# Second attention of a two-layer trunk: dividing by the softmax sums ahead of the transposes

## The chip, the cores and the metric

The kernel runs on one core of a Trainium2 chip. Its engines work from queues of their own, in order, and wait for each other by semaphores: TensorE (PE) multiplies matrices and transposes, VectorE (DVE) and ScalarE (ACT) do elementwise work, GpSimd (POOL) takes some of it, and SyncE (SP) starts transfers. The metric is the device time of one execution in microseconds (us), as the median of several runs.

## The reference

Two layers over 512 positions of width 1024; each has a token mixer and a gated MLP. The change is in the second layer's mixer, attention with 16 heads over a shared latent of width 128, limited to the 128 keys that an indexer picks for each query:

```python
def block(args):
    ...
    _, sel = lax.top_k(isc, topk)
    kg = k[bidx, sel]
    vg = vals[bidx, sel]
    logits = jnp.einsum('bqhd,bqkd->bqhk', qb, kg) * scale
    logits = logits + jnp.swapaxes(bias, -1, -2)
    logits = jnp.where(valid[:, :, None, :], logits, NEG)
    p = jax.nn.softmax(logits, axis=-1)
    return jnp.einsum('bqhk,bqkd->bqhd', p, vg)
...
o = jnp.einsum('bshl,hlv->bshv', o_lat, w_uv)
return o.reshape(B, S, DSA_HEADS * DSA_V_DIM) @ w_out
```

## The kernel before

The kernel keeps 512 positions on chip and streams the weights. Float32 products are made of three matmuls on split operands (a high and a low part). The second attention goes head by head. Queries of a head lie in four blocks j of 128, and block j needs only the first (j + 1) * 128 keys, so its tile `L[h, j]` has 128, 256, 384 or 512 columns.

For a head and a block these steps follow each other:

- `masked_bias` writes the scaled position bias into `L` (on ACT, on POOL for the two narrow blocks, on DVE for head 1) and POOL adds the mask (L1408). It runs two heads ahead.
- `logits` makes three matmuls into a PSUM tile `z` (L1421 to L1423).
- `softmax` adds `z` to `L` on DVE, with the row's least value as `nm` (L1431, two instructions: the operation and the read of its accumulator).
- `expo` takes the exponential on ACT in place and leaves the row sums in `sum` (L1436).
- `transposed` turns `L` on TensorE so that keys lie on partitions, in three groups: `tr` number 0 takes the first key block of all four tiles, number 1 and number 2 the rest (L1446). ACT copies number 0 into `pT` (L1451), DVE copies numbers 1 and 2 (L1453).
- `pair_values` projects the latent to the values of two heads, `weighted` multiplies a pair's transposed exponentials with them into the PSUM tile `av`, 64 partitions for each head (L1477).

The division by the sums comes last, for a pair of heads together. `av` has the value's columns on partitions and queries along the row, so the reciprocals have to lie along the row as well: `sums` takes the reciprocals, `pair_sums` spreads them over 64 columns on DVE (`rvb`, L1482), `pair_scale` transposes them in four matmuls (`bc`, L1491) and copies them to `bs` on ACT (L1493). `pair_hi` multiplies `av` by `bs` on DVE (L1497) and takes the high part on ACT (`ohi`, L1500); `pair_lo` subtracts for the low part on DVE (`olo`, L1504). The output projection uses both.

The order is the order in which the code is written; each engine's queue keeps it. Iteration h of the head loop makes logits and exponentials of head n = h + 1 and transposes head h, so `tr` of head h + 1 is the first use of what iteration h made. Between them `fill(k)` puts k steps (three matmuls of 512 columns each) of work from elsewhere, projections of the late heads' queries and later the output projection; `LATE_STEPS` says how many at three places of each iteration. In even iterations from 2 on, `weighted` of the pair before comes between the logits and the first transposes; in odd ones the first transposes follow right behind two blocks of logits.

Of the kernel before, what the change touches and what calls it, by code (L numbers as in the profile page):

```python
# [9 lines left out]
F32 = mybir.dt.float32  # L10
# [111 lines left out]
def kernel_body(ctx, tc, xT, wst, cst, smalls, crow, ccol, relb, onehot, outT):  # L122
# [959 lines left out]
    def dsa_layer(l, first, man):  # L1082
        with ExitStack() as st:
# [252 lines left out]
            with ExitStack() as sa:  # L1336
# [73 lines left out]
                def begin(h):  # L1410
                    if h % 2 == 0:
                        rv = ap.tile([P, QT, 2], F32, name="rv", bufs=4)
                        heads["rv"] = rv
                    heads[h] = (ap.tile([P, QT], F32, name="nm"), ap.tile([P, QT], F32, name="sum"), heads["rv"], {})

                def logits(h, j):
                    qh, ql = Q[h]
                    ns = (j + 1) * P
                    qs = slice(j * P, ns)
                    z = heads[h][3][j] = ptile([P, S], "z", "z")  # L1420
                    pe.matmul(z[:, :ns], lhsT=qh[:, qs], rhs=kph[:, :ns], start=True, stop=False)  # L1421
                    pe.matmul(z[:, :ns], lhsT=ql[:, qs], rhs=kph[:, :ns], start=False, stop=False)
                    pe.matmul(z[:, :ns], lhsT=qh[:, qs], rhs=kpl[:, :ns], start=False, stop=True)  # L1423

                def softmax(h, j):

                    nm, sum_, rv, z = heads[h]
                    z, L = z.pop(j), Ls[h, j]
                    ns = (j + 1) * P
                    c = h * QT + j  # L1430
                    dve.tensor_tensor_reduce(L, z[:, :ns], L, rq[:, c:c + 1], -USED, op0=OP.add, op1=OP.min,  # L1431
                                             accum_out=nm[:, j:j + 1])
# [47 lines left out]
                def pair_sums(rv):  # L1480
                    rvb = ap.tile([P, QT, 2, 64], F32, name="rvb", tag="bs")
                    dve.tensor_reduce(rvb, rv[:, :, :, None, None].to_broadcast([P, QT, 2, 64, 1]), axis=AX.X, op=OP.max)  # L1482
                    return rvb

                pair = {}

                def pair_scale(rvb):

                    bc = ptile([P, S], "bc", "x")
                    for j in range(QT):  # L1490
                        pe.transpose(bc[:, j * P:(j + 1) * P], rvb[:, j].rearrange("p a b -> p (a b)"), ident)  # L1491
                    bs = pair["bs"] = ap.tile([P, S], F32, name="bs")
                    act.activation(bs, bc, AF.Copy)  # L1493

                def pair_hi():
                    bs = pair["bs"]
                    dve.tensor_mul(bs, pair["av"], bs)  # L1497
                    oh = pp.tile([P, S], F32R, name="ohi", tag="qh", bufs=QRING)
                    ol = pp.tile([P, S], F32R, name="olo", tag="ql", bufs=QRING)
                    act.activation(oh, bs, AF.Copy)  # L1500
                    O.append((oh, ol))

                def pair_lo():
                    dve.tensor_sub(O[-1][1], pair["bs"], O[-1][0].bitcast(F32))  # L1504
# [14 lines left out]
                rvb = None  # L1519

                def sums(h):

                    dve.reciprocal(heads[h][2][:, :, h % 2], heads[h][1])
                    return pair_sums(heads[h][2]) if h % 2 else None

                for h in range(HEADS):
# [13 lines left out]
                    if more:  # L1540
                        softmax(n, 1)
                        expo(n, 1)
                    else:
                        rvb = sums(h)
                        pair_values(h - 1)
# [15 lines left out]
                    if values:  # L1561
                        pair_scale(rvb)
                    if more:
# [3 lines left out]
                        rvb = sums(h)  # L1567
# [10 lines left out]
                    if values:  # L1578
                        pair_hi()
                    elif h > 1:  # L1580
                        pair_lo()
                    fill(LATE_STEPS[h][2])
# [3 lines left out]
                    if not more:  # L1586
                        pair_scale(rvb)
# [135 lines left out]
```

## Time and profile before

| what | value |
|---|---|
| median of 3 runs | 1254.97 us (1254.44 to 1255.18) |
| profiled execution | 1254.88 us, its span from first to last instruction 1253.1 us |
| granted TensorE clock | 1.000 |
| busy: TensorE | 1241.6 us (99% of the span) |
| busy: weight loads of TensorE | 1015.6 us (81%) |
| busy: DVE | 929.8 us (74%) |
| busy: ACT | 607.4 us (48%) |
| busy: POOL | 119.7 us (10%), almost all between 743 and 854 us |

The second attention fills the stretch from about 743 to 866 us. A row of the timeline gives the start, the duration, the engine, the line, the operation, output and inputs with their shape, a count, and in brackets how long the engine had idled and for what. Successive operations of one engine may overlap by some hundredths of a microsecond, since a row begins before the row ahead has ended.

### The profile page before, as it was taken

Reading aid. Unit: us, or ns where it says so; the run is one execution under the profiler, and the core shown is the slowest. Engines: PE = TensorE matmul, PEld = TensorE weight load, DVE = VectorE, ACT = ScalarE, POOL = GpSimd, SP = SyncE. Lnnn points to the kernel's source line nnn. Section 1 sums busy time; section 2 is a strip of 40 time slices with the busy share of each in tenths; the row PEclk is TensorE's granted clock in tenths of the full one; section 3 lists DMA queues with packets and bytes.
Section 4 is the critical chain, followed back from the end, with each engine's and each line's share of the span. In section 5 each row is a group of like instructions: output and inputs, shape, how many; then the busy total and the mean of one; then the engine's idle time right before and its main releaser. Section 6 shows DMA issues by size and latency. Waiting matters only on the chain.

```text
span 1253.1 us, 16458 instructions
## 1 busy us (share of the span) xinstructions
PE 1241.6 (99%) x6138; PEld 1015.6 (81%) x6138; DVE 929.8 (74%) x1505; ACT 607.4 (48%) x1035; POOL 119.7 (10%) x127
## 2 busy tenths in 40 slices
PE   8999999999999999999999999999999999999998
PEld 5888787788888888888888778777888888888887
DVE  5889999798777877887788986666985455456653
ACT  6476676465323423343456447875654234234430
POOL 0000000000000000000001357773000000000000
PEclk9999999999999999999999999999999999999999
DMA  9734454413575576666322311141322422432231
GB/s 369 229 122 142 135 168 135 169 53 104 198 252 187 180 248 225 202 206 221 110 69 71 98 51 52 52 151 52 101 93 76 135 92 76 119 96 90 74 93 67
DMA packets 51327, 168.05 MB, mean 134 GB/s; under 512 B 6272, under 2 KB 7040, under 8 KB 51248
## 3 DMA queue, kind: packets, MB, share of 16 engines
q1 hardware_dynamic: 50816, 166.22, 40.9%
q8 instruction: 48, 0.79, 0.3%
q10 hardware_dynamic: 432, 0.79, 0.2%
q14 instruction: 31, 0.25, 0.1%
HBM read 164.84 MB, written 2.15 MB: 133 GB/s over the span
## 4 chain that ended last, share of the span: by engine, by line
PE 91%; DVE 4%; DMA 2%; ACT 1%; issue 1%; SPq 0%; DVEq 0%; POOL 0%; ACTq 0%
PE pt_u L252 12%; PE pt_u L253 12%; PE pt_u L254 12%; PE pt_d L253 5%; PE pt_d L252 5%; PE pt_d L254 5%; PE pt_q L252 2%; PE pt_l L252 2%; PE pt_l L254 2%; PE pt_l L253 2%; PE pt_q L254 2%; PE pt_q L253 2%; PE pt_first L252 2%; PE pt_first L254 2%; PE pt_first L253 2%; PE av L1477 1%
## 5 line engine op out<-in xcount | busy, mean ns | idle before, releaser
L211 ACT ACTIVATE whi<-raw 128x1024 fp32r<-128x1024 f32 (+1 forms) x206 | 205.0, 1002 | 110.4 <-PE pt_d L254 80.3
L252 PE MATMUL pt_u<-hhi,whi 128*128 128x512 f32 x640 | 249.2, 389 | 0.0
L253 PE MATMUL pt_u<-hhi,wlo 128*128 128x512 f32 x640 | 249.0, 389 | 0.0
L254 PE MATMUL pt_u<-hlo,whi 128*128 128x512 f32 x640 | 249.0, 389 | 0.0
L220 DVE TENSOR_TENSOR wlo<-raw,whi 128x1024 fp32r<-128x1024 f32 (+1 forms) x188 | 216.1, 1151 | 10.0 <-ACT whi L211 8.9
L995 ACT ACTIVATE y<-pt_u,sm 128x512 f32<-128x512 f32 x80 | 61.9, 777 | 180.5 <-PE pt_u L254 180.5
L252 PEld LDWEIGHTS pt_u<-hhi,whi 128*128 128x128 f32 x640 | 120.1, 188 | 26.1 <-issue 1.1
L254 PEld LDWEIGHTS pt_u<-hlo,whi 128*128 128x128 f32 x640 | 120.1, 188 | 24.9
L253 PEld LDWEIGHTS pt_u<-hhi,wlo 128*128 128x128 f32 x640 | 120.1, 188 | 24.8
L1000 DVE SCALAR_TENSOR_TENSOR y<-pt_u,sm,y 128x511 f32<-128x511 f32 x80 | 59.8, 748 | 92.7 <-ACT y L995 92.5
L254 PE MATMUL pt_d<-actlo,whi 128*128 128x512 f32 x288 | 112.0, 389 | 0.0
L252 PE MATMUL pt_d<-acthi,whi 128*128 128x512 f32 x288 | 112.0, 389 | 0.0
L253 PE MATMUL pt_d<-acthi,wlo 128*128 128x512 f32 x288 | 112.0, 389 | 0.0
L286 DVE SCALAR_TENSOR_TENSOR raw<-raw,cond 128x1024 f32<-128x1024 f32 x88 | 106.5, 1216 | 4.7 <-DMA raw<-wst 4.7
L371 DVE SCALAR_TENSOR_TENSOR x<-pt_d,mod,x 128x512 f32<-128x512 f32 x48 | 36.0, 749 | 67.1 <-PE pt_d L254 67.1
L236 ACT ACTIVATE acthi<-y 128x512 fp32r<-128x512 f32 x40 | 25.3, 632 | 94.2 <-DVE y L1018 94.2
L252 PEld LDWEIGHTS pt_d<-acthi,whi 128*128 128x128 f32 x288 | 54.1, 188 | 11.3
L254 PEld LDWEIGHTS pt_d<-actlo,whi 128*128 128x128 f32 x288 | 54.1, 188 | 11.2
L253 PEld LDWEIGHTS pt_d<-acthi,wlo 128*128 128x128 f32 x288 | 54.1, 188 | 11.2
L1001 DVE SCALAR_TENSOR_TENSOR y<-pt_u,sm,y 128x510 f32<-128x510 f32 x80 | 59.9, 749 | 2.8
L1431 DVE CUSTOM_DVE_ANT_0 L<-z,L,cols 128x128 f32<-128x128 f32 (+1 forms) x64 | 34.6, 547 | 32.2 <-PE tr L1446 22.0
L1201 POOL MEMSET work<- 128x128 f32 (+2 forms) x3 | 0.9, 308 | 585.8 <-PE pt_first L254 585.8
(307 smaller groups left out, 2561.2 us busy)
## 6 DMA issues: line engine op xcount, KB each, us to landing
raw<-wst SPq DMA_DIRECT2D x256, 512.0 KB, 3.7
raw<-wst SPq DMA_DIRECT2D x48, 384.0 KB, 3.1
th<-rb SPq DMA_DIRECT2D x16, 256.0 KB, 3.4
ada<-wst SPq DMA_DIRECT2D x4, 512.0 KB, 6.4
shrow<-shd SPq DMA_DIRECT2D x3, 512.0 KB, 3.7
outT<-x SPq DMA_DIRECT2D x6, 256.0 KB, 2.0
x<-xT SPq DMA_DIRECT2D x5, 256.0 KB, 5.1
x<-xT ACTq DMA_DIRECT2D x3, 256.0 KB, 3.9
```

What stands on the lines that cost most here:

```text
L211: act.activation(hi[:, :n], raw[:, :n], AF.Copy)
L220: engine.tensor_sub(lo[:, :w], raw[:, :w], hi[:, :w].bitcast(F32))
L236: act.activation(hi, src, AF.Copy)
L252: pe.matmul(out, lhsT=whi, rhs=ahi, start=start, stop=False)
L253: pe.matmul(out, lhsT=wlo, rhs=ahi, start=False, stop=False)
L254: pe.matmul(out, lhsT=whi, rhs=alo, start=False, stop=stop)
L286: dve.scalar_tensor_tensor(raw, raw, 1.0, cond, op0=OP.mult, op1=OP.mult, accum_out=dst)
L371: dve.scalar_tensor_tensor(x[f][:, c], pt, mod[l][:, g * KT + f:g * KT + f + 1], x[f][:, c], op0=OP.mult, op1=OP.add)
L995: act.activation(y, pt, AF.Identity, scale=cw[2], bias=sm[:, b + S_CB + c:b + S_CB + c + 1])
L1000: dve.scalar_tensor_tensor(y[:, 1:], pt[:, :S - 1], cw[1], y[:, 1:], op0=OP.mult, op1=OP.add)
L1001: dve.scalar_tensor_tensor(y[:, 2:], pt[:, :S - 2], cw[0], y[:, 2:], op0=OP.mult, op1=OP.add)
L1431: dve.tensor_tensor_reduce(L, z[:, :ns], L, rq[:, c:c + 1], -USED, op0=OP.add, op1=OP.min, accum_out=nm[:, j:j + 1])
```

## The change

The exponentials of a head are multiplied by the reciprocals of their sums on DVE, in place, before TensorE transposes them (`normed`). The reciprocals then are one number for each partition, and the spreading, its transposes, its copy and the product at the end of a pair fall away. `av` is split directly: `pair_hi` reads it from PSUM and moves to the place where `pair_scale` was, `pair_lo` follows in the same iteration. `normed` runs for the three narrow tiles behind the widest block's exponential, for the widest tile at the end of the iteration, and for all four tiles of head 0 ahead of the loop. `sum` gets four buffers.

```diff
                 def begin(h):
-                    if h % 2 == 0:
-                        rv = ap.tile([P, QT, 2], F32, name="rv", bufs=4)
-                        heads["rv"] = rv
-                    heads[h] = (ap.tile([P, QT], F32, name="nm"), ap.tile([P, QT], F32, name="sum"), heads["rv"], {})
+                    heads[h] = (ap.tile([P, QT], F32, name="nm"), ap.tile([P, QT], F32, name="sum", bufs=4), {})
...
-                def pair_sums(rv):
-                    rvb = ap.tile([P, QT, 2, 64], F32, name="rvb", tag="bs")
-                    dve.tensor_reduce(rvb, rv[:, :, :, None, None].to_broadcast([P, QT, 2, 64, 1]), axis=AX.X, op=OP.max)
-                    return rvb
-
                 pair = {}
 
-                def pair_scale(rvb):
-
-                    bc = ptile([P, S], "bc", "x")
-                    for j in range(QT):
-                        pe.transpose(bc[:, j * P:(j + 1) * P], rvb[:, j].rearrange("p a b -> p (a b)"), ident)
-                    bs = pair["bs"] = ap.tile([P, S], F32, name="bs")
-                    act.activation(bs, bc, AF.Copy)
-
                 def pair_hi():
-                    bs = pair["bs"]
-                    dve.tensor_mul(bs, pair["av"], bs)
...
-                    act.activation(oh, bs, AF.Copy)
+                    act.activation(oh, pair["av"], AF.Copy)
                     O.append((oh, ol))
 
                 def pair_lo():
-                    dve.tensor_sub(O[-1][1], pair["bs"], O[-1][0].bitcast(F32))
+                    dve.tensor_sub(O[-1][1], pair["av"], O[-1][0].bitcast(F32))
+
+                def normed(h, js):
+
+                    sum_ = heads[h][1]
+                    c = slice(js[0], js[-1] + 1)
+                    dve.reciprocal(sum_[:, c], sum_[:, c])
+                    for j in js:
+                        dve.tensor_scalar(Ls[h, j], Ls[h, j], sum_[:, j:j + 1], None, op0=OP.mult)
...
-                rvb = None
-
-                def sums(h):
-
-                    dve.reciprocal(heads[h][2][:, :, h % 2], heads[h][1])
-                    return pair_sums(heads[h][2]) if h % 2 else None
+                normed(0, range(QT))
 
                 for h in range(HEADS):
...
                     else:
-                        rvb = sums(h)
                         pair_values(h - 1)
...
                     if values:
-                        pair_scale(rvb)
+                        pair_hi()
                     if more:
                         logits(n, 3)
                         softmax(n, 3)
                         expo(n, 3)
-                        rvb = sums(h)
+                        normed(n, range(QT - 1))
...
                     if values:
-                        pair_hi()
-                    elif h > 1:
                         pair_lo()
+                    if more:
+                        normed(n, [QT - 1])
...
-                    if not more:
-                        pair_scale(rvb)
```

The order of the instructions shows three places. Names carry buffer numbers here; `L0` to `L3` are a head's four tiles, 128 to 512 columns wide. The queues of POOL and SP keep their order.

DVE in iteration 2, from the last logits step of head 3 to the first two of head 4. Before:

```order
L1431 ISA L3_6818,nm_6833<-z_6899,L3_6818,cols_5657 128x512
L1431 ISA nm_6833 128x1
L1523 RECIPROCAL rv_6748<-sum_6750 128x4
L1453 COPY pT_6859<-tr_6906 128x256
L1497 TENSOR_TENSOR bs_6897<-av_6845,bs_6897 128x512
L1431 ISA L0_6868,nm_6934<-z_6936,L0_6868,cols_5657 128x128
```

And now:

```order
L1428 ISA L3_6827,nm_6844<-z_6906,L3_6827,cols_5657 128x512
L1428 ISA nm_6844 128x1
L1492 RECIPROCAL sum_6845<-sum_6845 128x3
L1494 TENSOR_SCALAR L0_6779<-L0_6779,sum_6845 128x128
L1494 TENSOR_SCALAR L1_6800<-L1_6800,sum_6845 128x256
L1494 TENSOR_SCALAR L2_6824<-L2_6824,sum_6845 128x384
L1450 COPY pT_6870<-tr_6916 128x256
L1486 TENSOR_TENSOR olo_6904<-av_6856,ohi_6903 128x512
L1492 RECIPROCAL sum_6845<-sum_6845 128x1
L1494 TENSOR_SCALAR L3_6827<-L3_6827,sum_6845 128x512
L1428 ISA L0_6879,nm_6942<-z_6944,L0_6879,cols_5657 128x128
```

The widest multiply, which the first transposes of head 3 need, stands behind three multiplies, the copy of the last transposes and `olo`; the product with `bs` is gone.

DVE at the start, from head 0's last logits step to head 1's first. Before:

```order
L1431 ISA L3_6606,nm_6612<-z_6656,L3_6606,cols_5657 128x512
L1431 ISA nm_6612 128x1
L1403 TENSOR_SCALAR L3_6664<-th01_6512,cols_5657 128x512
L1431 ISA L0_6622,nm_6670<-z_6672,L0_6622,cols_5657 128x128
L1431 ISA nm_6670 128x1
```

And now:

```order
L1428 ISA L3_6606,nm_6611<-z_6655,L3_6606,cols_5657 128x512
L1428 ISA nm_6611 128x1
L1403 TENSOR_SCALAR L3_6663<-th01_6512,cols_5657 128x512
L1492 RECIPROCAL sum_6612<-sum_6612 128x4
L1494 TENSOR_SCALAR L0_6597<-L0_6597,sum_6612 128x128
L1494 TENSOR_SCALAR L1_6600<-L1_6600,sum_6612 128x256
L1494 TENSOR_SCALAR L2_6603<-L2_6603,sum_6612 128x384
L1494 TENSOR_SCALAR L3_6606<-L3_6606,sum_6612 128x512
L1428 ISA L0_6621,nm_6674<-z_6676,L0_6621,cols_5657 128x128
```

A reciprocal and four multiplies have come ahead of head 1's first logits step, and head 0's first transposes need them.

ACT in iteration 2, around the exponential of head 3's widest tile. Before:

```order
L1436 ACTIVATE L2_6815,sum_6834<-L2_6815,nm_6833 128x384
L1493 ACTIVATE bs_6897<-bc_6892 128x512
L1436 ACTIVATE L3_6818,sum_6834<-L3_6818,nm_6833 128x512
L1407 ACTIVATE L2_6910<-th_6732,cols_5657 128x384
L1407 ACTIVATE L3_6913<-th_6732,cols_5657 128x512
L1500 ACTIVATE ohi_6919<-bs_6897 128x512
```

And now:

```order
L1433 ACTIVATE L2_6824,sum_6845<-L2_6824,nm_6844 128x384
L1482 ACTIVATE ohi_6903<-av_6856 128x512
L1433 ACTIVATE L3_6827,sum_6845<-L3_6827,nm_6844 128x512
L1407 ACTIVATE L2_6920<-th_6739,cols_5657 128x384
L1407 ACTIVATE L3_6923<-th_6739,cols_5657 128x512
```

`ohi` has taken the place of the copy of `bs`, ahead of the exponential.

More of the change, by code (lines that the diff above doesn't have):

```diff
@@ L1419, in logits @@
                     qs = slice(j * P, ns)
-                    z = heads[h][3][j] = ptile([P, S], "z", "z")
+                    z = heads[h][2][j] = ptile([P, S], "z", "z")
                     pe.matmul(z[:, :ns], lhsT=qh[:, qs], rhs=kph[:, :ns], start=True, stop=False)
@@ L1425, in softmax @@
                 def softmax(h, j):
-                    nm, sum_, rv, z = heads[h]
+                    nm, sum_, z = heads[h]
                     z, L = z.pop(j), Ls[h, j]
```

## The prediction

> **What bounds the kernel now.** I read the table of windows first, to see which engine is full in the stage that the change touches. Columns: stretch, its length, busy time and count of TensorE (PE), its weight loads, VectorE (DVE), ScalarE (ACT), GpSimd (POOL), then granted clock and DMA.
>
> ```profile
> core 0: us, PE busy (x) PEld busy (x) DVE busy (x) ACT busy (x) POOL busy (x), PEclk, DMA share, GB/s
> 740.00:752.00 12.00, 10.29 (x59) 8.27 (x56) 8.99 (x30) 6.70 (x20) 8.09 (x11) 1.00 0.15 44
> 752.00:866.00 114.00, 113.19 (x718) 90.12 (x717) 74.93 (x205) 82.18 (x204) 80.39 (x89) 1.00 0.25 76
> ```
>
> From 752 to 866 us the second attention runs, and TensorE lacks 0.8 us of being always busy at full clock. So an operation taken off TensorE there is worth its own time, and any new wait of TensorE is lost at full price. Other engines have slack as a sum; what matters is when each hands over to TensorE.
>
> The chain of work and the group of the transposes price what is removed (start, time on the chain; group: busy us, mean ns):
>
> ```profile
> 766.33 0.44 PE bc L1491 x4
> L1491 PE MATMUL bc<-cons,rvb 128*128 128x128 f32 x32 | 4.8, 272 | 0.0
> ```
>
> Then I read the timeline, engine by engine, where one head hands over to the next. This is iteration 2, which makes head 3's exponentials while it transposes head 2; the last ACT rows and the POOL row start the bias of head 4. The 774 and 775 rows are an odd iteration, taken for spacing.
>
> ```profile
> 767.61 0.75 DVE L1431 CUSTOM_DVE_ANT_0 L<-z,L,cols 128x512 f32<-128x512 f32 x1 [0.35 <-PE tr L1446]
> 768.28 0.08 DVE L1431 DVE_READ_ACCUMULATOR2_ANT nm<- 128x1 f32 x1
> 768.40 0.72 ACT L1436 ACTIVATE L<-L,nm 128x512 f32<-128x512 f32 x1 [0.51 <-DVE nm L1431]
> 769.03 0.19 ACT L1436 ACTIVATION_READ_ACCUMULATOR L<-L,nm 128x1 f32 x1
> 769.12 1.22 ACT L1407 ACTIVATE L<-th,cols 128x384 f32<-128x384 f32 x2
> 769.58 0.60 PE L1446 MATMUL tr<-cons,L 128*128 128x128 f32 x4
> 769.80 2.05 POOL L1408 TENSOR_TENSOR L<-L,maskb 128x384 f32<-128x384 f32 x2 [1.80 <-ACT L L1407]
> ...
> 774.27 0.17 DVE L1523 RECIPROCAL rv<-sum 128x4 f32<-128x4 f32 x1
> 774.48 0.69 DVE L1482 TENSOR_REDUCE rvb<-rv 128x512 f32<-128x512 f32 x1
> 775.08 0.41 DVE L1453 COPY pT<-tr 128x256 f32<-128x256 f32 x1
> 775.41 0.68 DVE L1504 TENSOR_TENSOR olo<-bs,ohi 128x512 fp32r<-128x512 f32 x1
> ```
>
> Call S the end of VectorE's last logits step for the next head (768.28 + 0.08 = 768.36). The fourth of the next four transposes needs that head's widest tile; it starts 0.27 before the group's end, at 769.58 + 0.60 - 0.27 = 769.91, which is S + 1.55. The exponential (with its sum) is done at 769.22, S + 0.86. The hand-over has 0.7 us to spare now, and the change puts VectorE's work into it.
>
> **The change part by part.**
>
> 1. *Removed from TensorE:* 8 groups of four transposes, 0.44 us of the chain each: -3.5 us, all on the path. Their ACT copies (8) and DVE spreading and scaling (8 each, near 0.7 us) go as well, worth nothing by themselves, since TensorE's own work covers them. The same holds at the end of the stage, where the output projection's other matmuls keep TensorE busy while the last pair is split.
>
> 2. *Added on VectorE:* 64 multiplies of the exponentials and twice the reciprocals. No row shows this multiply in place; the nearest are one-input tensor-scalar operations in SBUF, first while GpSimd was idle, then beside it:
>
> ```profile
> L1244 DVE TENSOR_SCALAR maskb<-work 128x512 bf16<-128x512 f32 x1 | 0.4, 416 | 0.0
> L1244 DVE TENSOR_SCALAR maskb<-work 128x384 bf16<-128x384 f32 x1 | 0.3, 350 | 0.0
> L1244 DVE TENSOR_SCALAR maskb<-work 128x256 bf16<-128x256 f32 x1 | 0.3, 278 | 0.0
> ...
> 744.57 0.41 DVE L1403 TENSOR_SCALAR L<-th,cols 128x128 f32<-128x128 f32 x1
> 745.34 0.59 DVE L1403 TENSOR_SCALAR L<-th,cols 128x256 f32<-128x256 f32 x1
> 746.39 0.79 DVE L1403 TENSOR_SCALAR L<-th,cols 128x384 f32<-128x384 f32 x1
> ...
> 744.85 2.10 POOL L1408 TENSOR_TENSOR L<-L,maskb 128x384 f32<-128x384 f32 x2
> 745.73 2.37 POOL L1408 TENSOR_TENSOR L<-L,maskb 128x512 f32<-128x512 f32 x3
> ...
> 762.97 2.31 DVE L1161 SCALAR_TENSOR_TENSOR cols<-cols 128x16 f32<-128x16 f32 x1
> 762.85 2.40 POOL L220 TENSOR_TENSOR wlo<-raw,whi 128x1024 fp32r<-128x1024 f32 x1
> ...
> L1408 POOL TENSOR_TENSOR L<-L,maskb 128x384 f32<-128x384 f32 x14 | 12.9, 920 | 18.9 <-ACT L L1407 18.9
> ```
>
> Alone, 256, 384 and 512 columns take 0.28, 0.35 and 0.42 us: 0.07 per 128 columns, so 0.21 for 128. Beside GpSimd they take up to twice that. The 256-column one ends at 745.93, just after GpSimd went from its 384-wide operation to the next at 745.73; the tiny L1161 operation waits out a whole L220 operation, to 765.28 against 765.25. So such an operation waits until the GpSimd operation under way has ended. [...]
>
> 3. *The new order on VectorE in even iterations* (2 to 14): after S a reciprocal of three sums, three multiplies, the copy, the subtraction `olo` (moved here from the odd iteration), a reciprocal of the fourth sum, the widest multiply. The reciprocal starts at S - 0.08 and what depends on it 0.21 later (774.27 to 774.48): S + 0.13. Successive operations start about 0.08 before the row of the one ahead ends (0.69 long, 0.60 apart), so the multiplies take 0.13 + 0.20 + 0.27: S + 0.73; the copy 0.33 (775.08 to 775.41): S + 1.06; `olo` 0.60: S + 1.66; reciprocal 0.21: S + 1.87; multiply 0.42: S + 2.29; TensorE wakes 0.04 later (as ACT at 768.40): **S + 2.33** with a free port. But GpSimd's next bias operation starts at 769.80, S + 1.44, and holds on for 0.92, to S + 2.36. The multiply asks at S + 1.87, so it runs from there in about 0.28 (0.07 per 128 columns): S + 2.64, and TensorE goes on at **S + 2.68**. I take this, since the L1403 rows are the nearest kind and every one of them waited.
>
> Against it stands S + 1.55 in iteration 2. The other distances, two rows each (end of S; the transposes), for iterations 4, 6, 8 and 14:
>
> ```profile
> 783.96 0.08 DVE L1431 DVE_READ_ACCUMULATOR2_ANT nm<- 128x1 f32 x1
> 784.90 0.60 PE L1446 MATMUL tr<-cons,L 128*128 128x128 f32 x4
> 797.99 0.08 DVE L1431 DVE_READ_ACCUMULATOR2_ANT nm<- 128x1 f32 x1
> 798.61 0.69 PE L1446 MATMUL tr<-cons,L 128*128 128x128 f32 x4
> 811.35 0.08 DVE L1431 DVE_READ_ACCUMULATOR2_ANT nm<- 128x1 f32 x1
> 813.17 0.60 PE L1446 MATMUL tr<-cons,L 128*128 128x128 f32 x4
> 856.64 0.08 DVE L1431 DVE_READ_ACCUMULATOR2_ANT nm<- 128x1 f32 x1
> 858.62 0.60 PE L1446 MATMUL tr<-cons,L 128*128 128x128 f32 x4
> ```
>
> They are 1.19, 0.96, 2.07 and 2.23. Iteration 12 is built like 2, iteration 10 like 6 (one filler step behind the copy). New waits of TensorE with the port: 1.13 (2), 1.49 (4), 1.72 (6), 0.61 (8), 1.72 (10), 1.13 (12). Iteration 14 starts no more bias on GpSimd: 2.33 - 2.23 = 0.10. Iteration 0 has no `olo`, so its multiply comes ahead of GpSimd: 1.73 - 1.55 = 0.18. Sum **+8.0**; with a free port 0.78 + 1.14 + 1.37 + 0.26 + 1.37 + 0.78 + 0.10 + 0.18 = +6.0. Behind TensorE's wait everything in its queue waits, which is why I count it whole.
>
> 4. *Odd iterations:* after S TensorE still has the values' projection, the filler, the logits and the sixteen matmuls of the pair, several us, ahead of its transposes. The same VectorE steps without `olo` fit in: 0, unless GpSimd is late (a rival).
>
> 5. *The start:* head 0's four multiplies stand ahead of its first transposes with nothing between.
>
> ```profile
> 748.51 0.19 ACT L1436 ACTIVATION_READ_ACCUMULATOR L<-L,nm 128x1 f32 x1
> 748.36 0.72 PE L1446 MATMUL tr<-cons,L 128*128 128x128 f32 x4
> 748.06 2.23 POOL L1408 TENSOR_TENSOR L<-L,maskb 128x384 f32<-128x384 f32 x2
> ```
>
> The fourth transpose starts at 748.36 + 0.72 - 0.27 = 748.81 now. Sums are ready at 748.70; wake-up and reciprocal 0.25, multiplies 0.13 + 0.20 + 0.27 + 0.42, wake-up 0.04: 750.01, +1.2 with a free port. GpSimd runs two operations to 750.29; the first multiply can slip in between them, the second waits for the end: 750.29 + 0.14 + 0.27 + 0.42 + 0.04 = 751.1, **+2.3**, which I take.
>
> *Sum:* -3.5 + 8.0 + 2.3 = +6.8. The profiled execution took 1254.88 us (span 1253.1), 0.09 under the median of 1254.97: 1261.7 us.
>
> **The rivals.**
>
> *Free port:* the in-place multiply does not wait for GpSimd. Against it stand the L1403 rows; for it, that those read their input backwards. -3.5 + 6.0 + 1.2 = +3.7: 1258.6.
>
> *Taking turns:* each of the three multiplies in a row meets a fresh GpSimd operation, as L1161 met L220 0.12 after its start. In iteration 6 GpSimd is busy when they come:
>
> ```profile
> 797.38 0.92 POOL L1405 TENSOR_SCALAR L<-th,cols 128x256 f32<-128x256 f32 x1
> ```
>
> Each turn costs up to 0.92 us; some four more over the stage, or odd iterations spilling over: about +4 more, 1266. The table has GpSimd busy for 80.39 us of 114, so mostly its queue is not full. [...]
>
> *Hidden after all (other side):* VectorE gets to the widest multiply as soon as the exponential is out: S + 0.86 + 0.21 + 0.42 + 0.04 = S + 1.53. Then only iterations 4, 6 and 10 wait (0.34 + 0.57 + 0.57 = 1.5) and the start costs 1.2: -3.5 + 2.7 = -0.8, 1254.1, no change. It decides at the place of `olo` and the copy in VectorE's queue: they would have to be out of the way, and the order shows them ahead.
>
> *Plain gain:* the waits cost nothing, -3.5: 1251.4. The fourth multiply would have to end before S + 0.96, when the exponential is 0.1 us old; nearly excluded.
>
> **How the numbers follow.** A measurement of this kernel tells 0.2% (2.5 us) from no change. Forecast 0.60 (its own range 1259.5 to 1264), free port 0.18, taking turns 0.11, hidden 0.07, plain gain 0.04. Faster 0.04, same 0.07, slower 0.89. The range takes in the free port below and most of the turns above: 1257.5 to 1266.5.
>
> **What would show it.** In the changed trace: no `bc` group; in iterations 2 to 12 TensorE idle ahead of the fourth transpose, released by the multiply of L1494, 0.6 to 1.8 us each, least in 8 and 14; 128x512 multiplies longer than 0.42 us where a 128x384 operation of GpSimd runs, ending just after it; a gap of 2 us near 749; TensorE busy time down by 3.5 or more, the stage longer. It is wrong if these multiplies run beside GpSimd without waiting, if TensorE waits as much in odd iterations, or if it waits nowhere.

## The result and the profile after

The changed kernel takes 1267.67 us (median of 5 executions, 1266.35 to 1269.88), the kernel before beside it 1254.62 us (5 executions, 1254.32 to 1255.18): a ratio of 1.0102, 95% interval 1.0091 to 1.0113. It is slower, as forecast, but by 13 us and not by 6.8, and above the upper end of the range.

The profiled execution of the changed kernel is its slowest, 1269.88 us (span 1268.1). The stage, from the first logits matmul to the last group of transposes, has grown from 120.4 us (740.23 to 860.64) to 134.9 us (741.18 to 876.05). The table of windows, in two stretches as before (length; busy time and count of TensorE, its weight loads, VectorE, ScalarE, GpSimd; granted clock; DMA share, GB/s):

```profile
740.00:752.00 12.00, 8.54 (x47) 5.75 (x45) 10.59 (x30) 5.01 (x15) 7.16 (x9) 1.00 0.15 44
752.00:880.00 128.00, 118.82 (x699) 92.30 (x699) 88.47 (x270) 80.54 (x201) 82.86 (x90) 0.96 0.22 67
```

TensorE was short of being always busy by 0.8 us in the 114 us before; it now lacks 9.2 us in 128. And one column that stood at 1.00 everywhere before has moved: the granted clock is 0.96 over the stage. The waits of TensorE name the releaser (total us, times, longest):

```profile
PE tr L1443 <- DVE L L1494: 9.7, 11, 1.9
```

The `bc` group is gone. The timeline of iteration 2 is the place that the prediction worked out; S is now 774.17 + 0.09 = 774.26:

```profile
774.17 0.09 DVE L1428 DVE_READ_ACCUMULATOR2_ANT nm<- 128x1 f32 x1
774.17 0.17 DVE L1492 RECIPROCAL sum<-sum 128x3 f32<-128x3 f32 x1
774.38 0.88 DVE L1494 TENSOR_SCALAR L<-L,sum 128x128 f32<-128x128 f32 x3
775.17 0.42 DVE L1450 COPY pT<-tr 128x256 f32<-128x256 f32 x1
775.48 0.49 PE L1443 MATMUL tr<-cons,L 128*128 128x128 f32 x3
775.50 0.68 DVE L1486 TENSOR_TENSOR olo<-av,ohi 128x512 fp32r<-128x512 f32 x1
775.69 2.22 POOL L1408 TENSOR_TENSOR L<-L,maskb 128x384 f32<-128x384 f32 x2 [1.50 <-ACT L L1407]
776.10 0.16 DVE L1492 RECIPROCAL sum<-sum 128x1 f32<-128x1 f32 x1
776.29 0.59 DVE L1494 TENSOR_SCALAR L<-L,sum 128x512 f32<-128x512 f32 x1
776.94 0.33 PE L1443 MATMUL tr<-cons,L 128*128 128x128 f32 x1 [0.97 <-DVE L L1494]
```

The queue runs as predicted: three multiplies, copy, `olo`, reciprocal, widest multiply. Transposes start 0.11 apart, so the fourth was due at 775.48 + 0.33 = 775.81; it starts at 776.94, S + 2.68 as forecast, 1.13 late (0.97 of it shows as idleness).

Iterations 0 and 6 were worse than forecast. First 0, then 6:

```profile
759.59 2.22 POOL L1408 TENSOR_TENSOR L<-L,maskb 128x384 f32<-128x384 f32 x2 [2.14 <-DVE sum L1492]
759.60 1.19 DVE L1494 TENSOR_SCALAR L<-L,sum 128x512 f32<-128x512 f32 x1
760.84 0.33 PE L1443 MATMUL tr<-cons,L 128*128 128x128 f32 x1 [0.96 <-DVE L L1494]
...
804.69 0.92 POOL L1405 TENSOR_SCALAR L<-th,cols 128x256 f32<-128x256 f32 x1
805.20 1.39 DVE L1494 TENSOR_SCALAR L<-L,sum 128x128 f32<-128x128 f32 x3
805.70 2.83 POOL L1408 TENSOR_TENSOR L<-L,maskb 128x256 f32<-128x256 f32 x3
806.64 0.33 PE L1443 MATMUL tr<-cons,L 128*128 128x128 f32 x1 [0.39 <-DVE L L1494]
807.62 1.19 DVE L1494 TENSOR_SCALAR L<-L,sum 128x512 f32<-128x512 f32 x1
808.87 0.48 PE L1443 MATMUL tr<-cons,L 128*128 128x128 f32 x1 [1.90 <-DVE L L1494]
```

In iteration 0 the widest multiply begins 0.01 us behind a GpSimd operation and takes 1.19 us instead of about 0.5. In iteration 6 GpSimd works all but without a pause from 804.69 to 808.53, and both the three multiplies (1.39 against 0.88) and the widest (1.19) are stretched: TensorE waits in two places, 2.70 us in all.

The start, head 0's multiplies and transposes:

```profile
749.90 2.33 DVE L1494 TENSOR_SCALAR L<-L,sum 128x128 f32<-128x128 f32 x4
750.24 0.33 PE L1443 MATMUL tr<-cons,L 128*128 128x128 f32 x1 [0.77 <-DVE L L1494]
751.42 1.19 PE L1443 MATMUL tr<-cons,L 128*128 128x128 f32 x3 [0.85 <-DVE L L1494]
```

The fourth transpose starts at 751.42 + 1.19 - 0.27 = 752.34, against 748.81 before; the stage itself began 0.95 later in this execution (741.18 against 740.23), which leaves 2.6.

Last, the windows at less than the full clock, of 2 us each (the clock is the column behind POOL):

```profile
754.00:756.00 2.00, 2.00 (x10) 1.81 (x8) 0.40 (x1) 0.00 (x0) 0.23 (x1) 0.50 0.00 0
...
808.00:810.00 2.00, 1.13 (x4) 0.94 (x4) 1.49 (x5) 0.88 (x4) 1.71 (x3) 0.50 0.58 131
810.00:812.00 2.00, 2.00 (x8) 1.81 (x7) 0.27 (x1) 0.58 (x3) 0.10 (x1) 0.50 0.00 0
812.00:814.00 2.00, 2.00 (x9) 1.71 (x8) 1.19 (x4) 0.71 (x2) 1.49 (x2) 0.50 0.03 8
```

Windows of 0.2 us put the edges at 753.35 to 756.7 (3.4 us, behind the start's wait) and 807.9 to 814.7 (6.8 us, from inside iteration 6's wait). At half clock matmuls with 512 columns start 0.43 us apart (809.57 and 810.00) where they started 0.23 apart ahead of the drop (752.68 and 752.91), so about half of the time is lost, but only while TensorE has work: in the second stretch it goes on at 808.87, so 3.4 / 2 + (814.7 - 808.87) / 2 = 1.7 + 2.9 = 4.6 us.

So the profiled execution's +15.0 us (1269.88 against 1254.88) are: -3.5 (the `bc` transposes, by the forecast's row), +10.0 (waits ahead of the fourth transposes in the even iterations), +2.6 (start), +4.6 (clock), and 0.95 by which it came later into the stage; that makes 14.7, and 0.3 stay unassigned. The other four executions have mean clocks of 0.997 to 0.998 over their span where the profiled one has 0.996. Their traces were not taken, so where they lost it stays open. How much it was can be estimated: the median execution has 0.997, and 0.003 of its 1266 us are 3.8 us (0.6 more or less, since the clock is rounded). With that, -3.5 + 10.0 + 2.6 + 3.8 = +12.9, against the 13.05 us that were measured.

### The profile page after: what moved, and what is told of

Same layout as the page of the kernel before. It is cut to its first block, busy times and chain, and to the rows that moved or that the text cites. A ratio compares the mean times of both kernels' runs of the same rounds, so it can differ in the third digit from the quotient of the medians.

```text
span 1268.1 us, 16481 instructions
## 1 busy us (share of the span) xinstructions
PE 1246.4 (98%) x6106; PEld 1016.5 (80%) x6106; DVE 943.6 (74%) x1568; ACT 604.2 (48%) x1027; POOL 121.3 (10%) x127
## 4 chain that ended last, share of the span: by engine, by line
PE 88%; DVE 7%; DMA 2%; ACT 1%; issue 1%; SPq 0%; DVEq 0%; ACTq 0%; POOL 0%
PE pt_u L252 11%; PE pt_u L253 11%; PE pt_u L254 11%; PE pt_d L253 5%; PE pt_d L252 5%; PE pt_d L254 5%; PE pt_l L252 2%; PE pt_l L254 2%; PE pt_l L253 2%; PE pt_first L253 2%; PE pt_q L252 2%; PE pt_first L252 2%; PE pt_first L254 2%; PE pt_q L254 2%; PE pt_q L253 2%; PE av L1474 1%
```

## The experiments

The theory: (a) the multiplies stand in VectorE's queue between a head's logits and its transposes, and TensorE waits there; the queue's order and GpSimd's operations set how long; (b) the wait empties TensorE so far that its clock is halved behind it. Rivals: the multiplies cost in another way (GpSimd slowed by them, its bias late), or the clock drops for another reason.

In the table, "stage" is the time from the first logits matmul to the last group of transposes in the profiled execution, "waits" what TensorE's transposes waited for the multiplies. The ratio is to executions of before in the same set; their medians were 1254.62 us for the changed kernel, 1255.15 for the next four rows, 1255.66 for "both" to "three iterations" and 1255.48 for the last three. Before, too, loses some clock now and then: 17 of its 71 executions in the last three sets have a mean clock of 0.998 or 0.999.

| kernel | median us | ratio to before, 95% | stage us | waits us |
|---|---|---|---|---|
| changed | 1267.67 | 1.0102 (1.0091 to 1.0113) | 134.9 | 9.7 |
| no multiplies | 1251.52 | 0.9972 (0.9961 to 0.9983) | 117.4 | 0 |
| busy TensorE | 1265.49 | 1.0079 (1.0065 to 1.0093) | 130.8 | 1.8 |
| widest multiply first | 1259.85 | 1.0033 (1.0020 to 1.0045) | 123.6 | 3.1 |
| filler ahead | 1258.31 | 1.0021 (1.0012 to 1.0030) | 124.0 | 2.8 |
| both | 1256.38 | 1.0008 (1.0000 to 1.0017) | 121.6 | 1.3 |
| GpSimd's masks out | 1264.87 | 1.0078 (1.0064 to 1.0092) | 132.5 | 7.6 |
| one wait | 1256.77 | 1.0007 (0.9998 to 1.0016) | 123.3 | 3.0 |
| one multiplication, three iterations | 1253.01 | 0.9981 (0.9972 to 0.9990) | 117.6 | 0 |
| three waits | 1256.51 | 1.0009 (1.0000 to 1.0018) | 121.6 | 3.5 |
| both, `olo` later | 1254.17 | 0.9991 (0.9982 to 1.0000) | 119.7 | 0.8 |
| the same, more filler at the start | 1253.77 | 0.9985 (0.9976 to 0.9994) | 118.9 | 0.3 |

**No multiplies.** What is the removal worth alone?

```diff
-                    sum_ = heads[h][1]
-                    c = slice(js[0], js[-1] + 1)
-                    dve.reciprocal(sum_[:, c], sum_[:, c])
-                    for j in js:
-                        dve.tensor_scalar(Ls[h, j], Ls[h, j], sum_[:, j:j + 1], None, op0=OP.mult)
+                    return
```

> Leaves out the reciprocals and the multiplies of the exponentials (the output is not divided by the sums); everything else of the change stays. Theory (the loss is TensorE waiting for the multiplies, and its clock falling behind these waits): the removed transposes alone are left, -3.5 us, 1251.1 us, granted clock 1.000, no wait ahead of the fourth transpose. Rival (the moved ohi and olo, or the longer hold of av, cost as well): 1253 us or more.

Measured 1251.52 us, 3.6 under before (1255.15 beside it). The transposes no longer wait for VectorE, and no window of the stage is below the full clock. So the first term of the sum is right, and everything lost comes in with the multiplies: this is the floor of the other runs.

**Busy TensorE.** Useless matmuls of 128x512 into a free PSUM tile, just ahead of the transposes that wait.

```diff
+WARM = {0: 8, 1: 4, 3: 4, 5: 4, 7: 8, 11: 6, 13: 4}
...
+                def busy(n):
+                    if n:
+                        wz = ptile([P, S], "warmup", "x")
+                        for i in range(n):
+                            pe.matmul(wz, lhsT=kph[:, :P], rhs=kph, start=True, stop=True)
...
+                            if pi == 0 and j == (1 if h == 0 else QT - 1):
+                                busy(WARM.get(h, 0))
```

> The changed kernel with matmuls of no use (0.23 us each, into a free PSUM tile) put into TensorE's queue where it waits: 8 ahead of head 0's second transpose, 4 ahead of the fourth transpose in iterations 1, 3, 5 and 13, 8 in 7, 6 in 11. They fill most of each wait without lengthening it. Theory (behind the waits the granted clock falls to half for some us, and this costs 2.5 to 5 us on top): clock 1.000 throughout, 1264 us (1263 to 1265), runs closer together. Rival (the dips of the clock fall into time that is lost anyway, the waits alone make the difference): 1267 us or more, as before or worse.

Measured 1265.49 us (1264.68 to 1266.08), 0.5 above the top of the interval that the clock theory gave and under its rival's bound. The stretch behind the start's wait, which stood at 0.50 above, and the one in which iteration 6 ends (windows):

```profile
754.00:756.00 2.00, 2.00 (x14) 1.70 (x14) 1.52 (x4) 0.71 (x2) 1.37 (x2) 1.00 0.00 0
...
806.00:808.00 2.00, 1.93 (x10) 1.28 (x9) 1.75 (x5) 0.62 (x3) 1.92 (x3) 1.00 0.58 134
```

No window is below 1.00, and the kernel with more work on its fullest engine is 2.2 us faster. The waits are still spent, now as useless work. The stage is 4.1 us shorter, not 4.6: the added matmuls run some 0.5 us past the waits that they fill.

**Widest multiply first.**

```diff
                         normed(n, range(QT - 1))
+                        normed(n, [QT - 1])
...
-                    if more:
-                        normed(n, [QT - 1])
```

> The changed kernel with the widest multiply directly behind the three narrow ones, ahead of the copy of the last transposes and of olo on VectorE. Theory (the place in VectorE's queue sets the wait): it starts at S + 1.14, before GpSimd's wide operation at S + 1.43, TensorE goes on at S + 1.64, waits 0.1 in iterations 0, 2 and 12, 0.45 in 4, 0.7 in 6 and 10, none in 8 and 14: 2.1 us in place of 10; with the start 2.6 and one dip of the clock there 1.7: 1257.5 us (1256 to 1259). Rival (GpSimd holds the port whatever the place, or VectorE is simply full): waits near 1 us each stay, 1264 us or more.

Measured 1259.85 us, 7.8 under the changed kernel; 0.85 above the interval. In iteration 2 the queue is now (timeline):

```profile
773.30 0.88 DVE L1494 TENSOR_SCALAR L<-L,sum 128x128 f32<-128x128 f32 x3
774.09 0.16 DVE L1492 RECIPROCAL sum<-sum 128x1 f32<-128x1 f32 x1
774.28 0.49 DVE L1494 TENSOR_SCALAR L<-L,sum 128x512 f32<-128x512 f32 x1
774.40 0.76 PE L1443 MATMUL tr<-cons,L 128*128 128x128 f32 x4
774.61 2.06 POOL L1408 TENSOR_TENSOR L<-L,maskb 128x384 f32<-128x384 f32 x2 [1.50 <-ACT L L1407]
```

The multiply begins 0.33 ahead of GpSimd's operation, takes 0.49, and four transposes run as one group. So `olo` and the copy in front of it made the wait of iterations 2, 4 and 12. Waits are left at the start, in iteration 6 and, with 0.3 us in the row of idleness, in 10. What this profiled execution had at half clock lies at 10 to 16 us of the span, at the kernel's start, and not here; the one execution with a mean clock of 1.000 took 1257.84, inside the interval.

**Filler ahead.** The steps of the table that spreads projection work over the iterations, moved from behind the first transposes to ahead of them.

```diff
+for _h, _s in ((0, (2, 0, 2)), (1, (2, 0, 2)), (3, (2, 0, 2)), (5, (2, 0, 1)), (7, (1, 0, 2)), (9, (1, 1, 0)),
+               (11, (2, 0, 1)), (13, (2, 0, 2))):
+    LATE_STEPS[_h] = _s
```

> The changed kernel with filler steps moved from behind the first transposes to ahead of them, in iterations 0, 1, 3, 5, 7, 9, 11 and 13 (two steps, 1.4 us, in most; one in 7 and 9). No work added or left out. Theory (TensorE has work at hand that it could do meanwhile): waits fall to about 1.2 at the start, 2.0 in front of iteration 7, 0.4 of 11, the rest none, no dip of the clock: -3.5 + 3.6 = about 1255 us (1254 to 1257). Rival (the work is only late elsewhere, VectorE and GpSimd set the pace): waits come back behind, 1261 us or more.

Measured 1258.31 us, 1.3 above the interval. The useful work covers the waits of iterations 0, 2, 4, 8 and 12 without a change in VectorE's queue; in iteration 6, where one step was moved, 1.83 us stay, and behind them the clock is halved for 3.4 us (803.45 to 806.9). The expectation had that wait, with 2.0 us (it names it by head 7, whose transposes wait), but no dip of the clock. The profiled execution, the slowest of the ten, has a second dip at the kernel's start, at 11.6 to 15.0 us. The four executions with a mean clock of 1.000 took 1256.14 to 1257.07 us, which is the upper end of the interval.

**Both.** The two edits together.

> The changed kernel with both cures together: the widest multiply right behind the three narrow ones, and filler steps moved from behind the transposes to ahead of them. If the whole loss is TensorE's waits for the multiplies and the clock behind them, then with the order alone 3.1 us of waits were left (1.6 at the start, 1.2 in iteration 6, 0.3 in iteration 10), and the filler covers nearly all of it: at the floor without multiplies of 1251.5 plus about 0.5 at the start and 0.3 in iteration 6, 1252.3 us (1251.5 to 1254), faster than before, no stretch of the second attention at less than the full clock. Rival: the multiplies cost something beside the waits (the shared port slows GpSimd, the bias of the next heads comes late): 1255 or more.

Measured 1256.38 us: expected 1252.3, so it lies above its interval and within the rival's bound of 1255 or more. The theory was too simple, as the rival said, but the cost beside the waits that the trace shows is one that the rival didn't name: TensorE waits for more than the multiplies. The list of its waits:

```profile
PE z L1421 <- DVE nm L1431: 2.9, 3, 1.7
PE tr L1446 <- DVE L L1497: 1.3, 2, 0.8
```

1.7 us of the first row, a single wait, is in every kernel here, before too. The other 1.2 us are new: behind iterations 6 and 10 VectorE's first logits steps of the next head, queued behind multiply, copy and `olo`, free the PSUM tile of TensorE's logits too late. Against the stage without multiplies it is 4.2 us longer: 1.4 at the start, 2.2 in iteration 6, 0.5 in 10.

**GpSimd's masks out.** Do its operations make the multiplies long?

```diff
-                    pool.tensor_add(L, L, maskb[:, LOFF[j]:LOFF[j] + ns])
+                    if h < 2 or j < 2:
+                        pool.tensor_add(L, L, maskb[:, LOFF[j]:LOFF[j] + ns])
```

> The changed kernel without GpSimd's mask additions on the two wider tiles of heads 2 to 15 (their masks are left out of the computation). If GpSimd's hold on the shared port makes the multiplies long, the widest falls from up to 1.19 us to 0.5 wherever it met one, and the three narrow ones in iteration 6 from 1.39 to about 0.8: waits ahead of the fourth transpose of 0.4 in iteration 0 (from 1.13), 1.0 in 2, 4 and 12 (from 1.13), 1.6 in 6 and 10 (from 2.70 and 1.80), the start unchanged: 2 us less of waits, and up to 3.4 us less of clock, so 1262 to 1265.5 us against 1267.7. Rival: the multiplies are that long by themselves, or iteration 6 is late for another reason: 1267 or more, and multiplies of 1.2 us are still there.

Measured 1264.87 us (1263.11 to 1268.9), in the interval. Iteration 0, then iteration 6:

```profile
761.63 0.49 DVE L1495 TENSOR_SCALAR L<-L,sum 128x512 f32<-128x512 f32 x1
762.18 0.33 PE L1444 MATMUL tr<-cons,L 128*128 128x128 f32 x1 [0.26 <-DVE L L1495]
...
806.26 0.68 POOL L1409 TENSOR_TENSOR L<-L,maskb 128x256 f32<-128x256 f32 x1
806.29 1.31 DVE L1495 TENSOR_SCALAR L<-L,sum 128x128 f32<-128x128 f32 x3
```

The widest falls from 1.19 to 0.49 and the wait of iteration 0 from 1.13 to 0.43: GpSimd's operation had made the multiply long. All waits fall by 2.1 us (9.7 to 7.6), as expected. The three narrow ones of iteration 6 stay at 1.31, and not 0.8: the mask of a 256-wide tile, which was left in, starts 0.03 us ahead of them. The expected gain on the clock did not show in the profiled execution, the slowest of the five, which has drops at the kernel's start, behind the start's wait and behind iteration 6.

**One wait.** The kernel without multiplies, with three multiplications by 1.0 of the widest tile in iteration 6.

```diff
+TIMES = {7: 3}
...
+                    for _ in range(TIMES.get(h, 0) if len(js) == 1 else 0):
+                        dve.tensor_scalar(Ls[h, QT - 1], Ls[h, QT - 1], 1.0, None, op0=OP.mult)
```

> The changed kernel without its reciprocals and multiplies, but with three multiplications by 1.0 of the widest tile in iteration 6 alone: one wait W of TensorE of 2.0 to 4.0 us in one place (to be read from the trace); the output is not divided. Clock theory (the clock is granted by TensorE's busy share in a stretch of about 3.4 us): behind it the clock is halved for 3.4 or 6.8 us, so the time is 1251.5 + W + 1.7 to 3.4. Rival (the drop had another cause than the wait): 1251.5 + W, full clock.

The profiled execution (1257.94 us) has W = 2.99, and the windows behind it:

```profile
800.94 0.48 PE L1444 MATMUL tr<-cons,L 128*128 128x128 f32 x1 [2.99 <-DVE L L1492]
...
800.00:802.00 2.00, 1.06 (x3) 0.94 (x4) 1.56 (x5) 0.81 (x3) 1.78 (x3) 0.55 0.42 126
802.00:804.00 2.00, 2.00 (x8) 1.73 (x7) 0.19 (x1) 0.65 (x3) 0.02 (x1) 0.50 0.00 0
804.00:806.00 2.00, 2.00 (x8) 1.71 (x7) 1.18 (x4) 0.71 (x2) 1.57 (x2) 0.50 0.03 8
```

The eleven executions fall on three levels: 1254.12 to 1254.68 us (three, mean clock 1.000), 1256.49 to 1257.24 (five, 0.999), 1257.60 to 1258.51 (three, 0.997). Floor plus wait is 1251.5 + 3.0 = 1254.5; with half of 3.4 us more 1256.2, with half of 6.8 us 1257.9. The profiled execution stands on the third level, and its one drop in the stage, from 800.2 on, begins inside the wait; it has none at the kernel's start. Where the executions of the second level have theirs isn't shown. The next run, which has no such wait, has levels too: eight of eleven executions at 1.000 (1251.62 to 1253.09 us), two at 0.999 (1254.2) and one at 0.997 (1255.83). A part of the drops here may thus be at the kernel's start. But with the wait only three of eleven keep the full clock, and without it eight. So the same wait in the same program costs 2.9 us, its length, where the clock stays full, and 6.4 us in the profiled execution, where it drops.

**The same with less.** First one multiplication in each of iterations 2, 4 and 12 (`TIMES = {3: 1, 5: 1, 13: 1}`).

> The same, but one multiplication by 1.0 in each of iterations 2, 4 and 12: three waits of 0.9 to 1.3 us, some 3.1 us in all, 25 us or more apart or at least in different stretches of 3.4 us. Clock theory: none of them empties a stretch enough, the clock stays full: 1251.5 + the waits, about 1254.6. Rival (any wait drops the clock, or none does): 1251.5 + waits + 1.7 for each of them, near 1259; or no difference in kind from the single wait.

It missed its aim: no wait appeared, and the 1253.01 us lie below 1254.6, so it says nothing of the clock theory. Without the narrow multiplies the widest one asks at S + 0.89 and is done in 0.43; in working out its waits I had left the narrow ones in, about 1 us with their reciprocal. It shows that one multiply fits in the hand-over where four do not. Then three in each (`{3: 3, 5: 3, 13: 3}`):

> As the run with one wait, without reciprocals and multiplies (the output is not divided), but with three multiplications by 1.0 in each of iterations 2, 4 and 12, which are to make three waits of about 1.1, 1.5 and 1.1 us, some 3.8 us in all (to be read from the trace), where the run with one wait had 2.99 us in one place and took 1254.1 to 1254.7 at full clock, 1256.5 to 1257.2 with one stretch of 3.4 us at half clock, 1257.6 to 1258.5 with two. Clock theory (the busy share of a stretch of 3.4 us decides, and needs more than about 1.3 us of idleness in it): most executions at full clock, 1251.5 + waits = 1255.3 (1254.5 to 1256), with a drop no more frequent than without the waits. Rival (a drop follows from any wait, or from the sum of them): most executions with 1.7 to 5 us more, 1257 to 1260.

Now there are three waits of 1.16 us, in all:

```profile
PE tr L1444 <- DVE L L1492: 3.5, 3, 1.2
```

1256.51 us, 0.5 above the interval; the stage is 4.2 us longer than the floor's. Eight of the eleven executions have a mean clock of 1.000, and in the profiled one, which has 0.999, the drop is at 10 to 16 us, at the kernel's start. With one wait of 2.99 us it was three of eleven, with none eight of eleven. So waits of 3.5 us in three places, 16 us or more apart, leave the clock as it was, and 2.99 us in one place mostly do not. The two runs were made on different chips of the same kind; before keeps 1.000 in 20 of 26 executions on the first and in 19 of 27 on the second, so the chip isn't what sets them apart.

**Both, and `olo` moved on.** Behind the next iteration's second logits step, where VectorE is idle; one filler step more ahead in iteration 6.

```diff
                         softmax(n, 1)
                         expo(n, 1)
+                        if h % 2 and h > 1:
+                            pair_lo()
                     else:
+                        pair_lo()
...
-                    if values:
-                        pair_lo()
```

> The changed kernel with the widest multiply right behind the narrow ones, the filler ahead of the transposes (one step more in iteration 6), and the subtraction olo moved on into the next iteration's idle stretch of VectorE, behind its second logits step. With order and filler alone the stage was 4.2 us longer than without any multiplies: 1.4 us at the start, 2.2 in iteration 6, 0.5 in iteration 10. If those are the waits for VectorE's queue, iterations 6 and 10 fall to about 0.3 together and the start stays: 1251.5 + 1.7 = 1253.2 us (1252.5 to 1254.5), faster than before by 0.1 to 0.2%. Rival (the olo that holds its PSUM bank for longer makes the filler or the next head wait, or the loss was not the waits): 1255.5 or more.

1254.17 us, in the interval. By the stage, the start still costs 1.4 us, iteration 10 nothing, and iteration 6 0.9, where about 0.3 was expected for 6 and 10 together. Then a third filler step ahead at the start (`(0, (3, 0, 1))`). A step takes 0.70 us in the trace (749.65 to 750.35), and not the 1.1 that the expectation has:

> The same with a third filler step (1.1 us) ahead of the first transposes. If the start's loss of 1.4 us is TensorE's wait for head 0's multiplies, most of it is covered: 1252.2 us (1251.7 to 1253.5). Rival (the wait moves behind the filler, to the next hand-over): the same time as without it, 1253.2.

1253.77 us (1252.42 to 1254.69), ratio 0.9985 (0.9976 to 0.9994): 0.27 above its interval, and the stage 0.8 us shorter than without the step, so more than half of the start's loss is covered. This version's median is 13.9 us under that of the changed kernel and 1.7 us under that of before beside it (1255.48), a gain of 0.15%. Its stage from 752 us on:

```profile
752.00:862.00 110.00, 108.57 (x676) 85.70 (x677) 86.72 (x269) 80.13 (x200) 80.39 (x91) 1.00 0.24 78
```

## Why the prediction was right in its sign and wrong in its size

Its own sum, term by term (us), with what the profiled execution has:

| term | predicted | measured |
|---|---|---|
| transposes of the reciprocals | -3.5 | -3.6 (run without multiplies, against before) |
| iteration 0 | 0.18 | 1.13 |
| iterations 2, 4, 12 | 1.13, 1.49, 1.13 | 1.13, 1.13, 1.13 |
| iterations 6, 10 | 1.72, 1.72 | 2.70, 1.80 |
| iterations 8, 14 | 0.61, 0.10 | 0.64, 0.34 |
| odd iterations | 0 | 0 |
| start | 2.3 | 2.6 |
| granted clock | not in the sum | 4.6 |

*The step that failed* is "any new wait of TensorE is lost at full price". Full price was the lowest: behind the start's wait and iteration 6's the granted clock was 0.50, and two waits of 5.3 us brought 4.6 us more. The prediction had read a clock of 1.00 in both rows of before, and its sum has no term for it. That the drop follows from the wait is shown by the busy TensorE (clock full, time down though work was added) and by the one wait, put alone into the kernel without multiplies: the drop begins inside it, and three of eleven executions keep the full clock where eight do without it. Without the clock the measured terms make -3.5 + 10.0 + 2.6 = +9.1, or 1264.0 us, inside the range; with it the profiled execution lies outside. This is also why the range was too narrow above: it held the turns of GpSimd, and no case in which a wait costs more than its length.

*The mechanism was right:* the queue's order, S + 2.68 in iteration 2 to the hundredth, the delay by GpSimd, no loss in odd iterations, least in 8 and 14. No run shows a port that VectorE and GpSimd share, the term that the forecast's +8.0 and some expectations use; what the runs show in its place is that the widest multiply takes 1.19 us where a GpSimd operation is under way at its start in iterations 0 and 6, and 0.49 where none is (at 782.68 and 798.78, and in iteration 0 with the wide masks out). The widest multiply put first ended the wait of iterations 2, 4 and 12. The hundredth itself hides two errors. The multiply asked at 776.29, 0.16 later than forecast, and still ended at 776.88, which is what the forecast's reckoning from GpSimd's operation gives: 775.69 + 0.92 + 0.28 = 776.89. With the 0.49 us that it takes where no GpSimd operation is under way at its start, it would have ended at 776.78. So GpSimd costs 0.10 us there and not 0.35, and the queue 1.03 and not 0.78. The run without GpSimd's wide masks agrees: iteration 2 still waits 1.02 us, and its even iterations 7.6 us together (0.43, 1.02, 1.02, 1.69, 0.42, 1.70, 1.02 and 0.33). So the queue makes at most three quarters of the 10.0 us, since the narrow masks were still there.

*Mis-sized terms.* The waits sum to 10.0 against 8.0 (the prediction's own terms make 8.1, so its sum should read +6.9). The L1403 rows beside GpSimd were up to 2.3 times as long as alone (0.79 against 0.35), not twice. Three multiplies take 0.79 from their start to the copy's (774.38 to 775.17), not 0.60. All 64 by the line's row (shortest, median and longest in ns):

```profile
L1494 DVE TENSOR_SCALAR L<-L,sum x64: 285/415/1253, 749.9 to 873.8; 128x128 f32<-128x128 f32 x16, 128x256 f32<-128x256 f32 x16, 128x384 f32<-128x384 f32 x16, 128x512 f32<-128x512 f32 x16
```

The shortest of them takes 0.285 us where I had 0.21 for 128 columns, and 512 columns took 0.49 with no GpSimd operation under way at their start where I had 0.42: the L1244 rows were 0.07 too short for each. That 0.19 moved iteration 0's widest multiply from just ahead of GpSimd's operation to 0.01 behind it, which cost the 0.95. Its end there is what the same reckoning gives: 759.59 + 0.92 for the GpSimd operation + 0.28 = 760.79, and 759.60 + 1.19 = 760.79. The rival *free port*, that the multiply does not wait for GpSimd, falls with this and with the run without masks, though its queue is the larger part of the waits.

*Taking turns* came true in one place: iteration 6, +1.0. Its 1266 us is near the result by coincidence, since it has turns in four more places and no clock.

*Hidden* (1254.1) named the copy and `olo` as what decides. With the two out of the way of the widest multiply the time was 1259.85, not 1254.1: the stage was 6.2 us longer than without multiplies and not 2.7, with 2.6 at the start (the rival had 1.2) and 2.2 in iteration 6 (0.57). That the last two runs gave 1254.17 and 1253.77 is a coincidence with its number, since they have filler ahead of the transposes too.

## What to carry to other kernels

Where one engine is full, an operation taken off it is worth its time only if nothing is put into the hand-over that it depends on: here 3.5 us of matmuls less brought 12.6 us of waits. Look up in the timeline what room is left between the last producer and the consumer, list what stands in the producing queue, and move every operation that nobody there waits for (here `olo`) to a place where that engine is idle, and independent work of the full engine ahead of the hand-over. And price a long wait of TensorE in one place higher than its length, several short ones at their length: here 2.99 us in one place left the clock full in three executions of eleven, three waits of 1.16 us in eight.

## What the runs showed of the hardware

In the changed kernel the drops to 0.50 begin at 753.35 and 807.9, 54.6 us apart, and last 3.4 and 6.8 us. In the run without GpSimd's masks they begin at 752.16 and 810.18, 58.0 us apart. Both distances are multiples of 3.41 us (54.6 / 16 and 58.0 / 17), about the length of the shorter drop; a step of 3.41 us is an estimate from these two distances. Cut at that step, four windows of the changed kernel read (the two ahead of the drops; then the emptiest of the stage's others, and one that does not fit), and two of the run without masks, the second of which is ahead of a drop:

```profile
749.94:753.35 3.41, 2.05 (x8) 1.34 (x9) 2.96 (x8) 0.82 (x3) 2.48 (x4) 0.99 0.01 2
804.55:807.96 3.41, 1.94 (x12) 1.26 (x10) 3.34 (x10) 2.42 (x6) 3.19 (x5) 0.99 0.00 0
...
773.83:777.24 3.41, 2.44 (x16) 2.00 (x15) 3.34 (x13) 3.33 (x8) 1.91 (x3) 1.00 0.00 0
743.11:746.52 3.41, 1.72 (x9) 1.21 (x8) 2.39 (x10) 2.21 (x7) 1.73 (x3) 1.00 0.29 70
...
745.33:748.75 3.42, 2.08 (x10) 1.82 (x11) 2.49 (x9) 3.13 (x10) 2.96 (x4) 1.00 0.53 153
748.75:752.16 3.41, 2.02 (x11) 1.36 (x9) 3.03 (x7) 1.24 (x4) 3.41 (x5) 1.00 0.00 0
```

The two with TensorE busy for 2.05 and 1.94 us of 3.41 are followed by half clock; the changed kernel's with 2.44 and more, outside the drops, are not. The window at 743.11 has only 1.72 and no drop, and in the run without masks 2.08 brought none and 2.02 one, so TensorE's busy time is not the whole measure; what else counts stays open. That TensorE's busy share in a stretch of some 3.4 us sets the clock, as the expectations of the runs with one wait and with three have it, is thus the author's guess, which no run shows. Nor was it shown why, of eleven executions with the one wait, three have a clock of 1.000 and eight a lower one. The longest gap ahead of a drop was 1.90 us in the changed kernel and 1.83 with the filler ahead.
